# A down projection in Strassen form: ten instead of eight row chunks in each half, two direct chunks, two of the norms ahead of the last product

## The chip, the cores and the metric

One core of a Trainium2 chip runs the whole program. The metric is the device time of one launch in microseconds (us), median of several runs; the kernel before takes 1778.9 us (three runs, 1778.78 to 1779.9).

## What is computed

The reference is a decoder trunk of two layers on 512 tokens of width 1024, all in float32. Each layer is feed-forward, mixer, feed-forward, each followed by a layer norm:

```
def swiglu_ffn(x, w_gu, w_down):
    a, u = jnp.split(x @ w_gu, 2, axis=-1)
    return (jax.nn.silu(a) * u) @ w_down
...
    for l in range(DEPTH):
        x = layer_norm(DEEPNORM_ALPHA * x + 0.5 * swiglu_ffn(x, ffn1_w_gu[l], ffn1_w_down[l]), ln1_g[l], ln1_b[l])
        x = layer_norm(DEEPNORM_ALPHA * x + hybrid_mixer(x, ...), ln2_g[l], ln2_b[l])
        x = layer_norm(DEEPNORM_ALPHA * x + 0.5 * swiglu_ffn(x, ffn2_w_gu[l], ffn2_w_down[l]), ln3_g[l], ln3_b[l])
```

The change concerns the second matrix product of the feed-forward, `h @ w_down`: h is 512 tokens by 2816, w_down is 2816 by 1024. It stands four times in the program (two in each layer).

## The kernel before

**Products.** Every product of two float32 operands is made of three matmuls (`mm3`, lines 171 to 176): both operands are split into a rounded high part and a rest (`split`, line 162: a cast on ScalarE, then a subtraction on VectorE), and high by high, low by high and high by low are summed in PSUM.

**The down projection** (`ffn` from line 638, `down_items` from 348). Of the 22 chunks of 128 rows of w_down, the first 16 (`FIRST`, four `GROUPS` of two chunks in each half) go through Strassen's scheme in Winograd's form: contraction, output columns and tokens are each halved, and seven products (p2, p1, p5, p6, p3, p7, p4 in the order of the loop at 736) stand for eight. One product is four groups, and a group is 12 matmuls with 512 moving columns (`seventh`, 699). The last six chunks are multiplied directly, 24 matmuls a chunk: one ahead of product p4 (line 741), one behind it, and the last four (`TAIL`) token group by token group (756 to 761), 12 matmuls for each half of a token group's row, and behind each token group its norm (`norm`, 459).

**Operands.** The token side is combined in place in `hT` by VectorE (`fifth`, `third`) and split into four slots of `xh` and `xl`, which hold nothing else in this stage (`operand`, 649). The weight side: p2 reads its block from a raw buffer; for the others one tile R holds a block of w_down, and after a group's split GpSimd starts a DMA that adds the next block onto it (line 376, `accum_op=ALU.add`). So between two uses of one R piece there is a split, a DMA of 512 KB and the next split. There are four such sets in each projection: p1 to p5, p5 to p6, p6 to p4 and p3 to p7, with one DMA to a group.

**Order.** `Weights.pump` emits splits of weights up to six units ahead of their use. Everything else is put in order by the scheduler of the language when the program is built, and each engine runs its list in order. Four token groups (t = 0 to 3, 128 tokens each) have their own PSUM banks, two for each (`acc[t][0]`, `acc[t][1]`). The stage that follows needs the normed Y of a token group transposed (`to_xT`, 436: 8 transposes on TensorE, split on ScalarE and VectorE). It begins with the tokens of t = 0 and 1, so that the norms of t = 2 and 3 may finish under it.

Of the kernel before, what the change touches and what calls it, by code (L numbers as in the profile page):

```python
# [18 lines left out]
P = 128  # L19
# [8 lines left out]
SCALE = HD ** -0.5  # L28
TAIL = 4
GROUPS = 4  # L30
FIRST = 4 * GROUPS
SEVEN = (2, 3, 4, 5, 6, 7, 8, 9, 10)
UBUFS = 6
LOOK = 6
DELAY = (4, 3, 9, 9)
STEPS = ((4, 2, 2), (3, 2, 3), (3, 3, 2), (3, 2, 2))
# [59 lines left out]
class Trunk:  # L96
# [64 lines left out]

    def split(self, hi, lo, src, behind=None):
        a = self.nc.scalar.copy(hi, src)  # L163
        b = self.nc.vector.tensor_sub(lo, src, hi.bitcast(F32))  # L164
        if behind is not None:
            self.tc.add_manual_dep(b.ins, behind.ins.name, NOSYNC, reason="the reading goes first")
        if self.pin:
            self.tc.keep_in_program_order(a)
            self.tc.keep_in_program_order(b)
# [94 lines left out]
    def rows_item(self, w, r0, key, pools, heads=False):  # L264

        def load():
            v = self.raw().rearrange("p (c n) -> p c n", c=2)
            if heads:
                for kv in range(2):
                    q0 = kv * 256 + r0 // 2  # L270
                    self.nc.sync.dma_start(v[kv * HD : (kv + 1) * HD],
                                           w[q0 : q0 + P, :].rearrange("(c p) n -> p c n", p=HD))
            else:
                self.nc.sync.dma_start(v, w[r0 : r0 + 256, :].rearrange("(c p) n -> p c n", p=P))
            return v

        def cut(c):
            def go(v, hi, lo):
                self.split(hi, lo, v[:, c, :], self.reading if pools[c] == self.tail_units else None)
# [53 lines left out]
    def ffn_items(self, gu, down, key):  # L333
        items = []
        for fp in range(NFP):
            a = self.cols_item(gu, fp * 256, (key, "a", fp))
            u = self.cols_item(gu, DFF + fp * 256, (key, "u", fp))
            if fp == 0:
                items += [a[0], u[0], a[1], u[1]]
            else:  # L340
                items += self.seven_items(a, u) if fp in SEVEN else a + u
        rows = []
        for fp in range(FIRST // 2, NFP):
            late = [self.tail_units if fp * 2 + c >= NF - TAIL else None for c in range(2)]
            rows += self.rows_item(down, fp * 256, (key, "d", fp), late)
        return items + self.down_items(down, key, rows[0]) + rows[1:]

    def down_items(self, w, key, row):

# [3 lines left out]
        R = {}  # L353
        ms = range(GROUPS // 2)

        def rows(i, j, r, n):
            r0 = i * GROUPS * 256 + r
            return w[r0 : r0 + n, j * 512 : (j + 1) * 512].rearrange("(k p) c -> p k c", p=P)

        def begin(i, place, go):  # L360
            def f(*args):
                pool, tag = place()
                for m in ms:
                    R[i, m] = pool.tile([P, 4, 512], F32, tag=tag, name=self.nm("R"), bufs=2)
                    self.nc.sync.dma_start(R[i, m], rows(i, i, m * 512, 512))
                return go(*args)
            return f

        def cut(t, g, *more):
            def go(v, hi, lo):  # L370
                hv, lv = (t_.rearrange("p (k c) -> p k c", k=2) for t_ in (hi, lo))
                src = R[t, g // 2][:, g % 2 * 2 : g % 2 * 2 + 2, :]
                self.split(hv, lv, src)
                for i, j in more:
                    self.tc.keep_in_program_order(
                        self.nc.gpsimd.dma_start(src, rows(i, j, g * 256, 256), accum_op=ALU.add))  # L376
                return hv, lv
            return go
# [3 lines left out]

        p2 = []
        for m in ms:
            p2 += self.wide_item(w, 0, GROUPS // 2 + m, (key, "b", m))
# [103 lines left out]
    def ffn(self, g_, b, out=None):  # L489
        nc, tc, W = self.nc, self.tc, self.W  # L490
        with ExitStack() as ctx:
# [99 lines left out]
            for fp in range(NFP):  # L591
# [31 lines left out]
                if fp == NFP - 1:  # L623
                    early = W.take()
                    hv = [v.rearrange("p (g f t) -> p g f t", g=2, f=2) for v in early]
                    self.split(*(v.rearrange("p g f t -> p (g f) t") for v in hv), hT[:, 2 * GROUPS : 2 * GROUPS + 4, :256])
                if fp in SEVEN:
# [13 lines left out]

            slots = [0]

            def part(m, i, j):

                f = (j * GROUPS + 2 * m) * 2
                return hT[:, f : f + 4, i * 256 : (i + 1) * 256]

            def operand(src):

                k = slots[0] = (slots[0] + 2) % KC
                f = src.shape[1]
                hh, hl = (v[:, k : k + 2, :].rearrange("p k t -> p (k t)").rearrange("p (f t) -> p f t", f=f)
                          for v in (self.xh, self.xl))
                self.split(hh, hl, src)
                h = f // 2
                return [(hh[:, q * h : q * h + h], hl[:, q * h : q * h + h]) for q in range(2)]

            s1 = pool.tile([P, 4, 256], F32, tag="tlh", name=self.nm("s1"), bufs=TAIL)

            def fifth(m):

                a11, a21, a22 = part(m, 0, 0), part(m, 1, 0), part(m, 1, 1)
                nc.vector.tensor_sub(s1, a21, a22)
                nc.vector.tensor_sub(a21, a11, a21)
                nc.vector.tensor_sub(a11, s1, a11)
                return operand(s1)

# [5 lines left out]
            def operands():  # L674
                ms = range(GROUPS // 2)
                for m in ms[1:]:
# [9 lines left out]
                for m in ms:  # L686
                    yield from operand(part(m, 1, 0))
                chunks = operand(hT[:, FIRST : FIRST + 2, :])
                yield chunks[0]
                for m in ms:  # L690
                    yield from operand(part(m, 1, 1))
                yield chunks[1]
                for f in range(NF - TAIL, NF, 2):
                    room = pool.tile([P, 2, 2, 512], F32R, tag="hr", name=self.nm("hr"), bufs=2)
                    self.split(room[:, 0], room[:, 1], hT[:, f : f + 2, :], self.reading)
                    for q in range(2):
                        yield room[:, 0, q : q + 1], room[:, 1, q : q + 1]

# [17 lines left out]

            def chunk(f):
                u, h = W.get(), ahead.pop(0)
                ahead.append(next(split))
                for i, (t, q) in enumerate(((0, 0), (0, 1), (1, 0), (1, 1), (2, 1), (3, 1), (2, 0), (3, 0))):  # L720
                    down(f, u, h, t, q)
                    if i % 4 == 3:
                        self.step()
                W.done()

# [3 lines left out]
            def into(banks, t0, q, scale, sign=ALU.add):  # L729

                for i, b_ in enumerate(banks):
                    y = self.Y[:, t0 + i, q * 512 : (q + 1) * 512]
                    self.reading = nc.vector.scalar_tensor_tensor(out=y, in0=y, scalar=scale, in1=b_, op0=ALU.mult,
                                                                  op1=sign)

            for n, (banks, new, more) in enumerate((
# [3 lines left out]
                if n == 6:  # L740
                    chunk(FIRST)
                for g in range(GROUPS):
                    u, h = W.get(), ahead.pop(0)
                    ahead.append(next(split))
                    seventh(banks, u, h, new and g == 0)
                    if more and g == GROUPS - 1:
                        into(banks, *more)
                    W.done(2 if n == 0 and g == 1 else 1)
            for f in range(FIRST + 1, NF - TAIL):
                if f == FIRST + 1:  # L750
                    gb = self.load_ln(self.spool, g_, b, "S", 2)
                chunk(f)
            ahead += list(split)
            us = [W.get() for _ in range(TAIL)]
            self.pend = []
            for t in range(NT):
                for q in range(2):
                    for i in range(TAIL):
                        down(NF - TAIL + i, us[i], ahead[i], t, q)
                    self.step()  # L760
                self.norm(t, acc[t], gb, out, DELAY[t], (1.0 if t < 2 else ALPHA, 1.0))

# [387 lines left out]
```

## Time and profile before

| what | value |
|---|---|
| median of three runs | 1778.9 us (1778.78 to 1779.9) |
| the profiled execution | 1778.04 us |
| its span, first to last instruction | 1776.3 us |
| TensorE busy | 1764.0 us, 99% |
| VectorE busy | 1385.9 us, 78% |
| ScalarE busy | 906.9 us, 51% |
| GpSimd busy | 162.4 us, 9% |
| granted TensorE clock, mean | 0.999 |
| HBM traffic | 117 GB/s over the span |

PE is TensorE, DVE VectorE, ACT ScalarE, POOL GpSimd, SP the engine that only issues DMAs. L174 is line 174 of the kernel. A matmul's row gives its modelled duration, which overlaps with the next one; the spacing of the starts is the rate. A VectorE instruction's duration overlaps with the next start in the same way. In a row of the timeline the bracket at the end is the idle time ahead of it on its engine and what ended it.

### The profile page before, as it was taken

The numbers are of one execution on the slowest core, as the hardware profiler recorded it, in microseconds if no ns is written. First come the engines' busy times: TensorE is split into PE (matmuls) and PEld (weight loads), VectorE is DVE, ScalarE is ACT, GpSimd is POOL, SyncE is SP. The second block draws the span as 40 slices with busy tenths as digits, with TensorE's granted clock in tenths as the row PEclk, the third lists the DMA queues.
The fourth block names the chain that finished last, engine by engine and source line by source line (L and its number), as shares of the span: only waits on it lengthen the run. The fifth ranks groups of instructions, "written<-read, shape, count | busy, mean of one in ns | idle before, by whom it ended". The sixth has DMA issues, their size and how long they took to land. (4 is left out here: it accounts for less than half of the span.)

```text
span 1776.3 us, 29093 instructions
## 1 busy us (share of the span) xinstructions
PE 1764.0 (99%) x11978; PEld 1609.5 (91%) x11978; DVE 1385.9 (78%) x1927; ACT 906.9 (51%) x1424; POOL 162.4 (9%) x136
## 2 busy tenths in 40 slices
PE   9999999999999999999999999999999999999998
PEld 9999988887789999998899999889877899999886
DVE  7788888756757788879788887877567587888795
ACT  5455565278712455556235555643795234555550
POOL 0000031111111000012000000301011110000221
PEclk9999999999999999999999999999999999999999
DMA  6234396323222243288412334962233122234871
GB/s 190 96 103 135 120 226 154 113 84 90 74 75 72 84 131 96 96 235 154 156 50 96 117 96 156 225 165 66 84 96 95 48 95 96 96 100 138 226 151 51
DMA packets 158326, 210.07 MB, mean 118 GB/s; under 512 B 4848, under 2 KB 116208, under 8 KB 158192
## 3 DMA queue, kind: packets, MB, share of 16 engines
q1 hardware_dynamic: 140784, 174.64, 30.5%
q0 software_dynamic: 17408, 33.56, 10.6%
q8 instruction: 94, 1.54, 0.4%
q14 instruction: 40, 0.33, 0.1%
HBM read 206.09 MB, written 2.10 MB: 117 GB/s over the span
## 5 line engine op out<-in xcount | busy, mean ns | idle before, releaser
L174 PE MATMUL ps<-xh,uh 128*128 128x256 f32 (+1 forms) x1616 | 482.2, 298 | 0.0
L176 PE MATMUL ps<-xh,ul 128*128 128x256 f32 (+1 forms) x1616 | 479.4, 297 | 0.3 <-DVE ul L164 0.2
L175 PE MATMUL ps<-xl,uh 128*128 128x256 f32 (+1 forms) x1616 | 478.9, 296 | 0.7 <-DVE xl L164 0.5
L163 ACT CAST uh<-raw 128x1024 fp32r<-128x1024 f32 (+1 forms) x286 | 248.3, 892 | 259.1 <-PE ps L175 140.0
L164 DVE TENSOR_TENSOR ul<-raw,uh 128x1024 fp32r<-128x1024 f32 (+1 forms) x286 | 286.5, 1021 | 69.7 <-ACT uh L163 69.1
L174 PE MATMUL ps<-Th,uh 128*128 128x256 f32 x1152 | 319.1, 277 | 0.0
L175 PE MATMUL ps<-Tl,uh 128*128 128x256 f32 x1152 | 318.7, 277 | 0.0
L176 PE MATMUL ps<-Th,ul 128*128 128x256 f32 x1152 | 318.3, 276 | 0.0
L174 PEld LDWEIGHTS ps<-xh,uh 128*128 128x128 f32 x1616 | 308.0, 191 | 9.8 <-issue 1.6
L176 PEld LDWEIGHTS ps<-xh,ul 128*128 128x128 f32 x1616 | 307.9, 191 | 9.4 <-DVE ul L164 0.9
L175 PEld LDWEIGHTS ps<-xl,uh 128*128 128x128 f32 x1616 | 308.0, 191 | 9.1 <-DVE xl L164 1.7
L174 PE MATMUL ps<-uh,xh 128*128 128x512 f32 x672 | 264.3, 393 | 0.5 <-ACT xh L163 0.5
L176 PE MATMUL ps<-uh,xl 128*128 128x512 f32 x672 | 262.0, 390 | 0.0
L175 PE MATMUL ps<-ul,xh 128*128 128x512 f32 x672 | 261.6, 389 | 0.0
L163 ACT CAST uh<-S 128x1024 fp32r<-128x1024 f32 x144 | 151.1, 1050 | 149.1 <-PE ps L175 145.2
L164 DVE TENSOR_TENSOR ul<-S,uh 128x1024 fp32r<-128x1024 f32 x144 | 175.9, 1222 | 60.0 <-ACT uh L163 59.3
L174 PEld LDWEIGHTS ps<-Th,uh 128*128 128x128 f32 x1152 | 216.7, 188 | 0.0
L175 PEld LDWEIGHTS ps<-Tl,uh 128*128 128x128 f32 x1152 | 216.7, 188 | 0.0
L176 PEld LDWEIGHTS ps<-Th,ul 128*128 128x128 f32 x1152 | 216.4, 188 | 0.0
L376 POOL DMA_DIRECT2D R<-in_ffn_w_down_dram x64 | 77.8, 1221 | 983.0 <-DVE ul L164 952.2
L174 PEld LDWEIGHTS ps<-uh,xh 128*128 128x128 f32 x672 | 126.2, 188 | 28.2 <-issue 1.6
L176 PEld LDWEIGHTS ps<-uh,xl 128*128 128x128 f32 x672 | 126.1, 188 | 27.3 <-DVE xl L164 0.9
(143 smaller groups left out, 2388.7 us busy)
## 6 DMA issues: line engine op xcount, KB each, us to landing
raw<-in_ffn_w_gu_dram SPq DMA_DIRECT2D x86, 1024.0 KB, 5.7
R<-in_ffn_w_down_dram POOLq DMA_DIRECT2D x64, 512.0 KB, 7.3
raw<-in_ffn_w_down_dram SPq DMA_DIRECT2D x20, 1024.0 KB, 5.0
raw<-in_w_in_dram SPq DMA_DIRECT2D x18, 1024.0 KB, 5.2
R<-in_ffn_w_down_dram SPq DMA_DIRECT2D x16, 1024.0 KB, 6.4
raw<-in_w_in_dram SPq DMA_DIRECT2D x8, 512.0 KB, 5.1
raw<-in_w_out_dram SPq DMA_DIRECT2D x8, 512.0 KB, 6.1
raw<-in_w_out_dram SPq DMA_DIRECT2D x4, 1024.0 KB, 5.0
```

The costliest lines, as they stand in the source:

```text
L163: a = self.nc.scalar.copy(hi, src)
L164: b = self.nc.vector.tensor_sub(lo, src, hi.bitcast(F32))
L174: keep(mm(out, ah, bh, start=start, stop=False, **kw))
L175: keep(mm(out, ah, bl, start=False, stop=False, **kw))
L176: keep(mm(out, al, bh, start=False, stop=stop, **kw))
L376: self.nc.gpsimd.dma_start(src, rows(i, j, g * 256, 256), accum_op=ALU.add))
```

## The change

`GROUPS` goes from 4 to 5, so that 20 chunks take the seven products and two (`TAIL`) are direct. A half of ten chunks is handled in three pieces of 4, 4 and 2 chunks (`PAIRS`). The accumulating DMAs become five to a set, 20 instead of 16 in each projection. The two direct chunks of token groups 0 and 1 and their norms now stand ahead of p4, and those of token groups 2 and 3 behind it. The norm's two vectors are loaded at the start of the projection, into its own pool. The line that held one reading of PSUM ahead of a split (`behind`) goes. In the changed kernel the lines are shifted: split is 163 to 166, the accumulating DMA 374, the norm 485 to 497, the reading of a product's banks 747.

```diff
-TAIL = 4
-GROUPS = 4
-FIRST = 4 * GROUPS
+TAIL = 2
+GROUPS = 5
+HALF = 2 * GROUPS
+FIRST = 2 * HALF
+PAIRS = [(m, min(4, HALF - m)) for m in range(0, HALF, 4)]
...
-DELAY = (4, 3, 9, 9)
+DELAY = (5, 4, 9, 9)
...
-        return items + self.down_items(down, key, rows[0]) + rows[1:]
+        return items + self.down_items(down, key, tail)
...
+        def plain(m):
+            k0, n = PAIRS[m]
+
+            def load():
+                v = self.raw()[:, : n * 512].rearrange("p (k c) -> p k c", k=n)
+                self.nc.sync.dma_start(v, rows(1, 0, k0, n))
+                return v
...
+        p2 = [item for m in range(len(PAIRS)) for item in plain(m)]
         p1, p5, p6, p4 = product(0, (0, 1)), product(0, (1, 1)), product(0, (1, 0)), product(0)
         p3, p7 = product(1, (0, 1)), product(1)
-        p2[2] = p2[2][:3] + (begin(0, lambda: (self.spool, "S"), p2[2][3]),)
-        p5[0] = p5[0][:3] + (begin(1, lambda: (self.fpool, "hr"), p5[0][3]),)
-        return p2 + p1 + p5 + p6 + p3 + p7 + [row] + p4
+        for m in range(2):
+            hook(p2, 2, 0, m, lambda: (self.spool, "S"))
+            hook(p5, 0, 1, m, lambda: (self.fpool, "hr"))
+        hook(p1, 1, 0, 2, lambda: (self.fpool, "r"))
+        hook(p5, 0, 1, 2, lambda: (self.fpool, "r"))
+        return p2 + p1 + p5 + p6 + p3 + p7 + tail + p4
...
+            gb = self.load_ln(pool, g_, b)
+            calls = [0]
...
-                k = slots[0] = (slots[0] + 2) % KC
+                calls[0] += 1
+                k, h = ((4, 0), (0, 0), (0, 1), (4, 1))[calls[0] % 4 if calls[0] < 20 else 2]
                 f = src.shape[1]
-                hh, hl = (v[:, k : k + 2, :].rearrange("p k t -> p (k t)").rearrange("p (f t) -> p f t", f=f)
-                          for v in (self.xh, self.xl))
+                hh, hl = (v[:, k : k + f, h * 256 : (h + 1) * 256] for v in (self.xh, self.xl))
                 self.split(hh, hl, src)
...
+            def tail(t):
+                for q in range(2):
+                    for i, (u, h) in enumerate(last):
+                        down(FIRST + i, u, h, t, q)
+                    self.step()
+                self.norm(t, acc[t], gb, out, DELAY[t], (1.0 if t < 2 else ALPHA, 1.0))
...
                 if n == 6:
-                    chunk(FIRST)
+                    last = [take() for _ in range(TAIL)]
+                    self.pend = []
+                    for t in range(2):
+                        tail(t)
                 for g in range(GROUPS):
...
-            for f in range(FIRST + 1, NF - TAIL):
-                if f == FIRST + 1:
-                    gb = self.load_ln(self.spool, g_, b, "S", 2)
-                chunk(f)
-            ahead += list(split)
-            us = [W.get() for _ in range(TAIL)]
-            self.pend = []
-            for t in range(NT):
-                for q in range(2):
-                    for i in range(TAIL):
-                        down(NF - TAIL + i, us[i], ahead[i], t, q)
-                    self.step()
-                self.norm(t, acc[t], gb, out, DELAY[t], (1.0 if t < 2 else ALPHA, 1.0))
+            for t in range(2, NT):
+                tail(t)
```

On TensorE the built program has 11422 rows where the one before has 11470.

What VectorE runs at three places, in its order. In the names `ul` is the low part of a weight unit, `raw` a weight buffer filled by DMA, `R` the accumulated tile, `xl` the low part of a token-side operand or of the transposed input, `ps` a PSUM bank, `Y` the residual stream, `ln` the norm's vectors, `S` a sum of weights for the next feed-forward.

First place: VectorE around the last product of the first feed-forward. Before:

```order
L164 TENSOR_TENSOR ul_3301<-raw_3238,uh_3300 128x1024
L164 TENSOR_TENSOR ul_3320<-raw_3238,uh_3319 128x1024
L164 TENSOR_TENSOR ul_3339<-raw_3286,uh_3338 128x1024
L164 TENSOR_TENSOR ul_3373<-raw_3286,uh_3372 128x1024
L164 TENSOR_TENSOR ul_3380<-raw_3323,uh_3379 128x1024
L164 TENSOR_TENSOR ul_3384<-raw_3323,uh_3383 128x1024
L164 TENSOR_TENSOR ul_3390<-raw_3376,uh_3389 128x1024
L164 TENSOR_TENSOR ul_3607<-raw_3376,uh_3606 128x1024
L466 SCALAR_TENSOR_TENSOR Y<-Y,ps_2780 128x512
L468 BN_STATS st_3417<-Y 128x6
L466 SCALAR_TENSOR_TENSOR Y<-Y,ps_2781 128x512
```

Now:

```order
L166 TENSOR_TENSOR ul_3368<-R_2828,uh_3367 128x1024
L747 SCALAR_TENSOR_TENSOR Y<-Y,ps_2785 128x512
L747 SCALAR_TENSOR_TENSOR Y<-Y,ps_2787 128x512
L166 TENSOR_TENSOR ul_3424<-raw_2772,uh_3423 128x1024
L485 SCALAR_TENSOR_TENSOR Y<-Y,ps_2781 128x512
L485 SCALAR_TENSOR_TENSOR Y<-Y,ps_2782 128x512
L487 BN_STATS st_3385<-Y 128x6 x2
L485 SCALAR_TENSOR_TENSOR Y<-Y,ps_2783 128x512
L489 BN_AGGR mv_3390<-st_3385 128x2
```

The norm of token group 0 stood behind all splits of the stage and six splits of the next one; now it stands behind the readings of p7 (L747) and the last split of p4's weights (R_2828), and the splits of the next stage's weights (raw_2772 and later) stand between the steps of the norms.

Second place: VectorE where a feed-forward follows a feed-forward, at the norm of token group 3. Before:

```order
L475 SCALAR_TENSOR_TENSOR Y<-Y,mv_8992,ln_8774 128x1024
L582 SCALAR_TENSOR_TENSOR hT_9012<-ps_9022,Q_9071 128x256
L478 SCALAR_TENSOR_TENSOR Y<-Y,rs_8996,ln_8774 128x1024
L306 TENSOR_TENSOR S_9341<-raw_9019 128x512
L310 TENSOR_TENSOR S_9341<-raw_9019 128x512
```

Now:

```order
L306 TENSOR_TENSOR S_9379<-raw_8992 128x512
L489 BN_AGGR mv_9036<-st_9031 128x2
L310 TENSOR_TENSOR S_9379<-raw_8992 128x512
L491 TENSOR_SCALAR ve_9038<-mv_9036 128x1
L494 SCALAR_TENSOR_TENSOR Y<-Y,mv_9036,ln_8241 128x1024
L307 TENSOR_TENSOR S_9379<-S_9379,raw_8992 128x512
L497 SCALAR_TENSOR_TENSOR Y<-Y,rs_9040,ln_8241 128x1024
```

Three of the sums S now stand ahead of the last step of that norm (L497, before L478); they stood behind it.

Third place: VectorE at the end of the program, where the two last norms begin. Before:

```order
L475 SCALAR_TENSOR_TENSOR Y<-Y,mv_17710,ln_17611 128x1024
L466 SCALAR_TENSOR_TENSOR Y<-Y,ps_17062 128x512
L478 SCALAR_TENSOR_TENSOR Y<-Y,rs_17714,ln_17611 128x512 x2
L468 BN_STATS st_17745<-Y 128x6
L466 SCALAR_TENSOR_TENSOR Y<-Y,ps_17063 128x512
```

Now:

```order
L494 SCALAR_TENSOR_TENSOR Y<-Y,mv_17748,ln_17122 128x1024
L497 SCALAR_TENSOR_TENSOR Y<-Y,rs_17752,ln_17122 128x512 x2
L485 SCALAR_TENSOR_TENSOR Y<-Y,ps_17118 128x512
L487 BN_STATS st_17833<-Y 128x6
L485 SCALAR_TENSOR_TENSOR Y<-Y,ps_17119 128x512
```

The first reading for token group 2 (ps_17062, now ps_17118) stood inside the norm of token group 1; now that norm is finished ahead of it. The two last norms themselves are laced into each other as before.

## Rows read from the trace of the kernel before

**Rows 1.** The page: the span, and part 1, busy time by engine.

```profile
span 1776.3 us, 29093 instructions
...
PE 1764.0 (99%) x11978; PEld 1609.5 (91%) x11978; DVE 1385.9 (78%) x1927; ACT 906.9 (51%) x1424; POOL 162.4 (9%) x136
```

**Rows 2.** Groups by line and shape: a 512-column matmul, busy us, mean ns, idle time ahead.

```profile
L174 PE MATMUL ps<-uh,xh 128*128 128x512 f32 x672 | 264.3, 393 | 0.5 <-ACT xh L163 0.5
```

**Rows 3.** Timeline of PE: first and last of the program's last 96 matmuls.

```profile
1746.28 0.39 PE L174 MATMUL ps<-uh,hr 128*128 128x512 f32 x1
...
1767.83 0.39 PE L176 MATMUL ps<-uh,hr 128*128 128x512 f32 x1
```

**Rows 4.** Busy time by stretch: the first down projection, clock, DMA share, GB/s.

```profile
core 0: us, PE busy (x) PEld busy (x) DVE busy (x) ACT busy (x) POOL busy (x), PEclk, DMA share, GB/s
234.00:345.00 111.00, 111.00 (x507) 92.41 (x506) 92.14 (x98) 49.82 (x52) 24.13 (x19) 1.00 0.72 170
```

**Rows 5.** Timeline of DVE: two splits back to back, and the next start.

```profile
264.69 2.35 DVE L164 TENSOR_TENSOR xl<-hT,xh 128x1024 fp32r<-128x1024 f32 x2
266.96 1.22 DVE L164 TENSOR_TENSOR ul<-R,uh 128x1024 fp32r<-128x1024 f32 x1
```

**Rows 6.** Timeline of DVE: the end of the program.

```profile
1749.21 0.69 DVE L466 SCALAR_TENSOR_TENSOR Y<-Y,ps 128x512 f32<-128x512 f32 x1 [12.99 <-PE ps L176]
...
1760.37 0.68 DVE L466 SCALAR_TENSOR_TENSOR Y<-Y,ps 128x512 f32<-128x512 f32 x1
1760.96 1.41 DVE L478 SCALAR_TENSOR_TENSOR Y<-Y,rs,ln 128x512 f32<-128x512 f32 x2
1762.29 0.69 DVE L468 BATCH_NORM_STATS2 st<-Y 128x6 f32<-128x512 f32 x1
...
1765.84 0.68 DVE L466 SCALAR_TENSOR_TENSOR Y<-Y,ps 128x512 f32<-128x512 f32 x1
...
1771.83 1.42 DVE L478 SCALAR_TENSOR_TENSOR Y<-Y,rs,ln 128x512 f32<-128x512 f32 x2 [0.44 <-POOL rs L474]
```

**Rows 7.** Timeline of PE: the first matmul of the first down projection.

```profile
232.39 0.39 PE L174 MATMUL ps<-uh,uh 128*128 128x512 f32 x1
```

**Rows 8.** Timeline of POOL: the accumulating DMAs of the first projection (16 in all).

```profile
236.24 1.35 POOL L376 DMA_DIRECT2D R<-in_ffn_w_down_dram  x1 [234.93 <-DVE ul L164]
...
240.75 1.20 POOL L376 DMA_DIRECT2D R<-in_ffn_w_down_dram  x1 [1.05 <-DVE ul L164]
246.43 1.23 POOL L376 DMA_DIRECT2D R<-in_ffn_w_down_dram  x1 [4.48 <-DMA R<-in_ffn_w_down_dram]
...
277.74 1.22 POOL L376 DMA_DIRECT2D R<-in_ffn_w_down_dram  x1 [0.98 <-DVE ul L164]
```

**Rows 9.** Line 376: issue to landing of the 64 accumulating DMAs.

```profile
DMA to landing us min/median/max: 5.7/7.3/11.2
```

**Rows 10.** DMA, 210 to 290 us in 40 slices of 2 us.

```profile
DMA  9996808729328999999999999999999999999300
GB/s 274 401 369 194 330 1 219 305 33 348 152 33 289 406 391 306 247 214 208 209 202 210 201 214 204 182 204 207 200 183 200 204 201 195 205 201 199 73 0 0
```

**Rows 11.** DMA issues, 222 to 262 us: KB each, median us to landing.

```profile
R<-in_ffn_w_down_dram SPq DMA_DIRECT2D x2, 1024.0 KB, 9.2
```

**Rows 12.** The page, part 6: the same loads over the whole program.

```profile
R<-in_ffn_w_down_dram SPq DMA_DIRECT2D x16, 1024.0 KB, 6.4
```

**Rows 13.** Timeline of DVE where a feed-forward follows a feed-forward.

```profile
897.85 1.28 DVE L478 SCALAR_TENSOR_TENSOR Y<-Y,rs,ln 128x1024 f32<-128x1024 f32 x1
899.17 0.69 DVE L306 TENSOR_TENSOR S<-raw 128x512 f32<-128x512 f32 x1
899.78 0.68 DVE L310 TENSOR_TENSOR S<-raw 128x512 f32<-128x512 f32 x1
```

**Rows 14.** Timeline of PE at the same place: 256-column matmuls, then transposes.

```profile
900.10 0.28 PE L174 MATMUL ps<-xh,uh 128*128 128x256 f32 x1
...
901.54 1.91 PE L442 MATMUL ps<-ident,Y 128*128 128x128 f32 x16
```

More of the change, by code (lines that the diff above doesn't have):

```diff
@@ L160, in units, with split @@
         return hi, lo
-    def split(self, hi, lo, src, behind=None):
+    def split(self, hi, lo, src):
         a = self.nc.scalar.copy(hi, src)
         b = self.nc.vector.tensor_sub(lo, src, hi.bitcast(F32))
-        if behind is not None:
-            self.tc.add_manual_dep(b.ins, behind.ins.name, NOSYNC, reason="the reading goes first")
         if self.pin:
@@ L278, in go @@
             def go(v, hi, lo):
-                self.split(hi, lo, v[:, c, :], self.reading if pools[c] == self.tail_units else None)
+                self.split(hi, lo, v[:, c, :])
                 return hi, lo
@@ L375, in go @@
                     self.tc.keep_in_program_order(
-                        self.nc.gpsimd.dma_start(src, rows(i, j, g * 256, 256), accum_op=ALU.add))
+                        self.nc.gpsimd.dma_start(src, rows(i, j, g * 2, 2), accum_op=ALU.add))
                 return hv, lv
@@ L625, in ffn @@
                     hv = [v.rearrange("p (g f t) -> p g f t", g=2, f=2) for v in early]
-                    self.split(*(v.rearrange("p g f t -> p (g f) t") for v in hv), hT[:, 2 * GROUPS : 2 * GROUPS + 4, :256])
+                    self.split(*(v.rearrange("p g f t -> p (g f) t") for v in hv), hT[:, HALF : HALF + 4, :256])
                 if fp in SEVEN:
@@ L674, in operands @@
             def operands():
-                ms = range(GROUPS // 2)
+                ms = range(len(PAIRS))
                 for m in ms[1:]:
@@ L687, in operands @@
                     yield from operand(part(m, 1, 0))
-                chunks = operand(hT[:, FIRST : FIRST + 2, :])
-                yield chunks[0]
+                room = pool.tile([P, 2, TAIL, 512], F32R, tag="hr", name=self.nm("hr"), bufs=2)
+                self.split(room[:, 0], room[:, 1], hT[:, FIRST:, :])
+                for q in range(TAIL):
+                    yield room[:, 0, q : q + 1], room[:, 1, q : q + 1]
                 for m in ms:
                     yield from operand(part(m, 1, 1))
[L692 to L695, printed above, removed]
-                    for q in range(2):
-                        yield room[:, 0, q : q + 1], room[:, 1, q : q + 1]
             def seventh(banks, u, h, new):
@@ L715, in ffn, with take @@
             ahead = [(hv[0][:, g], hv[1][:, g]) for g in range(2)] + [next(split)]
-            def chunk(f):
+            def take():
                 u, h = W.get(), ahead.pop(0)
[L719 to L722, printed above, removed]
-                        self.step()
-                W.done()
+                ahead.append(next(split, None))
+                return u, h
             low, high = [acc[t][0] for t in (2, 3)], [acc[t][1] for t in (2, 3)]
@@ L740, in ffn @@
                 if n == 6:
-                    chunk(FIRST)
+                    last = [take() for _ in range(TAIL)]
+                    self.pend = []
+                    for t in range(2):
+                        tail(t)
                 for g in range(GROUPS):
-                    u, h = W.get(), ahead.pop(0)
-                    ahead.append(next(split))
+                    u, h = take()
                     seventh(banks, u, h, new and g == 0)
```

55 lines of the change are left out of this document (28 added, 27 removed).

## The prediction, on record ahead of the result

> **What bounds the kernel now.** I read the share of busy time first: TensorE is busy 1764.0 of 1776.3 us, VectorE 1385.9, the rest far less [rows 1]. An average does not say whether TensorE is also never kept waiting, so next come the groups by line: the 672 high-by-high matmuls with 512 columns have 0.5 us of idle time ahead of them in the whole program [rows 2]. [...] So every matmul taken away is worth its spacing, as long as what feeds TensorE keeps its lead. Two things could lose it: VectorE, with 18.9 us to spare in 111, and the accumulating DMAs, during which the DMA engines are at nine tenths or more from about 236 to 284 us [rows 10]. The one place where TensorE does not set the time is the end of the program, so I read VectorE's timeline there too [rows 6].
>
> **The matmuls.** Four more direct chunks go into the scheme. They took 4 x 24 = 96 matmuls; as a fifth group in each of seven products they take 7 x 12 = 84. That is 12 fewer in a projection, 48 in the program, as the row counts on TensorE say (11470 to 11422). The spacing comes from the last 96 matmuls: 1767.83 - 1746.28 = 21.55 us for 95 steps, 0.2268 us [rows 3]. So 12 x 0.2268 = 2.72 us a projection and **-10.9 us** in all, while no new wait appears. A group of 12 takes 2.72 us; a product takes 13.6 instead of 10.9, seven take 95.3.
>
> **VectorE inside the projection.** In units of 1024 elements: weight splits rise by 7 x 1 and fall by 4 (direct chunks), 3 more; operand splits go from 17 to 18.5; the combinations in `fifth` and `third` go from 2 pieces to 2.5 at four operations each, 2 more. These 6.5 start every 1.14 us ((266.96 - 264.69) / 2, [rows 5]): 7.4 us more on an engine with 18.9 us idle, in a stage 2.7 us shorter. The norms of token groups 0 and 1 were in the stage before and still are. VectorE is left with some 9 us idle and has no queue that grows; cost nothing, covered by TensorE's own 95 us.
>
> **The norms ahead of p4.** One norm occupies VectorE for 1765.84 - 1760.37 = 5.47 us [rows 6]. Two need 10.9 us; p4 behind the direct chunks gives 13.6 us. What waits on VectorE behind these norms is the split of p4's last operand piece, used in its fifth group, and the next stage's splits. By VectorE's order and these durations the piece's split comes some 11 us behind the readings of p7, and TensorE needs it 5.4 + 4 x 2.72 = 16.3 us behind them. Cost nothing; without the cover it is the 5 us between.
>
> **Accumulating DMAs.** Each projection issues 20 instead of 16 on POOL. The 16 took from 236.24 to 277.74, 2.77 us each, three in flight at a time (the fourth, at 246.43, waited for a landing) [rows 8]; the last lands a median 7.3 us after issue [rows 9], at 285.0. Product p7, which needs the last set, began at 232.39 + 5 x 10.9 = 286.7 [rows 7], its last group 8.2 us later, and a group's split should be done 2.2 us ahead (a cast and a subtraction): a lead of about 8 us. After the change the first issue is some 3.5 us later (239.8; VectorE has three more operations of 1.14 us ahead of it), the last 19 steps on, 239.8 + 19 x 2.77 = 292.4, landed at 299.7. The last group of p7 begins at 232.39 + 5 x 13.6 + 10.9 = 311.3; its limit is 309: a lead of 9.4 us. Against this stand loads that the change brings into the stretch: the next stage's first 1 MB of weights, 1 MB of norm vectors and three 0.5 MB pieces where there were none, about 3.1 MB; at the 400 GB/s that plain loads reach [rows 10] 7.8 us. All of that lateness in one chain leaves 1.6 us. So the cost is nothing at the lower end; at the upper, with the 3.4 us a step of the first three issues (246.43 - 236.24, [rows 8]) kept up for all 19, the last lands at 311.7, 2.7 us late in each projection. I take nothing, since 12 of the 15 steps were at the faster rate.
>
> Plain loads and accumulations do share: the two R loads issued among the accumulations took 9.2 us [rows 11], against 6.4 over the program [rows 12]. [...]
>
> **The boundaries.** Behind the last two direct parts (24 matmuls, 5.4 us) the next stage starts on tokens whose transposes were made inside p4. After a feed-forward the next one runs 96 matmuls of 256 columns at 0.12 us ((901.54 - 900.10) / 12, [rows 14]), 11.5 us, before it transposes token groups 2 and 3: 16.9 us from the start of those direct parts. VectorE reads the first of their banks after 6 matmuls and 0.21 us (1.57 us; the 0.21 from 1749.21 - 1746.28 - 12 x 0.2268, [rows 3, 6]), works two norms (10.9) plus their last step (1.3), and three sums of 0.61 us [rows 13] that now stand ahead of that step: 15.6. Splits of the next weights ahead of them can hold VectorE for one or two operations more, 16.7 to 17.9. Before, the norm was done at 899.13 and the transposes began at 901.54 [rows 13, 14], 2.4 us of slack. I take **+0.4 us** for this one boundary (bounds 0 and 2). Towards the mixer there are 24 more matmuls between, 2.9 us: nothing, twice.
>
> **The end of the program.** Before, the last direct matmul is issued at 1768.06 and the span ends at 1776.3: 8.2 us exposed. After, the last 24 matmuls take 5.44 us, the first reading starts 1.57 us into them, and from the reading of token group 2 to the last L478 the trace has 1771.83 + 1.42 - 1760.37 = 12.88 us, of which 1.33 (1762.29 - 1760.96) belong to the norm before it, now finished earlier: 11.55. Behind the last step come 3.05 us of output [rows 6]. 1.57 + 11.55 + 3.05 = 16.2 us, 10.7 of them exposed: **+2.5 us**. Bounds: nothing, if the two norms hid as before, and one norm, 5.5.
>
> **Sum.** -10.9 + 0.4 + 2.5 = -8.0 us. The profiled execution took 1778.04 us, 0.9 below the median of 1778.9; against the median I forecast **1770.9 us**, 0.45% less.
>
> **The rivals.**
> Full gain: the end costs nothing more because the two last norms are laced more tightly. Then -10.9, 1768.0 us. For it: POOL and TensorE leave VectorE free there. Against: VectorE is solid in the last 24 us [rows 6], with two norms and only 5.4 us of matmuls to hide them.
> Partly lost: the norms of token groups 2 and 3, or the accumulations, are late by 0.5 to 2 us at several of the places with little lead. With 1 us in each of four projections -4, 1774.9; with 2 us at the three boundaries -2, 1776.9. For it: leads of 1.6 and about 0 us. Against: those leads add every unfavourable bound.
> Slower: the accumulating DMAs become the bound of p7. Each step of i us lands the last at 239.8 + 19i + 7.3; TensorE waits 19i - 61.9 us in each projection, and the gain of 8.0 / 4 = 2.0 us is gone at i = 3.36. At 3.6 it waits 6.5 us in each, 26 in all: 1797 us. For it: 3.4 us a step while plain loads ran. Against: 2.61 in the 12 steps behind them, since 277.74 - 246.43 = 31.3 [rows 8].
> That the change doesn't do what it says is excluded by the row count on TensorE.
>
> **The numbers.** The forecast 0.64, full gain 0.08, partly lost 0.20, slower 0.08. The range from 1767.6 to 1776.0 holds the first two, the forecast's bounds (end 0 to 5.5, boundary 0 to 2) and about half of the partly lost. A measurement here tells 0.2% from no change, 3.6 us. Faster by more: 0.64 + 0.08 + half of 0.20 = 0.82. Same: the other half and 0.01 of the slower case, 0.11. Slower: 0.07.
>
> **What would show it.** Right: the spacing stays at 0.227 us, TensorE is busy without a gap through seven products of 13.6 us, each projection is 2.7 us shorter, the last L497 ends about 7.6 us behind the last matmul's issue, where it was 5.2. Wrong: a wait of TensorE for a split `ul` of an R tile with a DMA behind it (the accumulations), or for transposes of token groups 2 and 3 (the boundaries), or POOL steps above 3.3 us.

## The result, and the profile after

The changed kernel takes 1785.25 us (median of six runs, 1782.59 to 1788.07) against 1779.16 us for the kernel before on the same chip (six runs, 1778.78 to 1779.9): a ratio of 1.0033, 95% interval 1.002 to 1.0046, 6.1 us **slower**. The forecast was 1770.9 us, and its range ended at 1776.0. The profiled execution took 1784.17 us, 6.1 more than the one before. Two single runs of later kernels, one of `e6_transposes_later` (2919.5 us, granted clock 0.56) and one of `e8_four_ahead` (1916.7 us, 0.85), ran in a slow state and are no part of the comparisons.

The first view below answers to [rows 1]. The second is the group of 512-column matmuls whose token side is a low part (`xl`); its columns are those of [rows 2].

```profile
span 1782.4 us, 29182 instructions
...
PE 1758.7 (99%) x11930; PEld 1603.4 (90%) x11930; DVE 1414.1 (79%) x1975; ACT 926.9 (52%) x1456; POOL 181.8 (10%) x152
```

```profile
L176 PE MATMUL ps<-uh,xl 128*128 128x512 f32 x720 | 283.2, 393 | 9.3 <-DVE xl L166 9.3
```

TensorE's matmuls fell as forecast (11978 to 11930), but in front of one group of them it stood 9.3 us, waiting for VectorE's `xl`. The timeline of PE shows where: in the third product, p5, of each projection, at its fifth group, the one whose token-side operand is the new 2-chunk piece.

```profile
271.06 0.39 PE L175 MATMUL ps<-ul,xh 128*128 128x512 f32 x1
274.15 0.50 PE L176 MATMUL ps<-uh,xl 128*128 128x512 f32 x1 [2.70 <-DVE xl L166]
...
275.83 0.63 PE L176 MATMUL ps<-uh,xl 128*128 128x512 f32 x1
276.26 0.63 PE L174 MATMUL ps<-uh,xh 128*128 128x512 f32 x1
```

The other three projections have the same row with waits of 2.73, 3.19 and 0.68 us. Behind the wait the spacing is 0.43 us instead of 0.227. Busy time by stretch, in the columns of [rows 4], shows that the granted clock has fallen to 0.50:

```profile
272.00:274.00 2.00, 0.00 (x0) 0.00 (x0) 1.73 (x2) 1.45 (x3) 0.66 (x2) 1.00 1.15 209
274.00:276.00 2.00, 1.85 (x7) 1.54 (x8) 2.00 (x3) 2.00 (x3) 1.15 (x1) 0.85 1.12 205
276.00:278.00 2.00, 2.00 (x7) 1.51 (x6) 2.00 (x3) 1.30 (x2) 1.22 (x1) 0.50 1.12 205
278.00:280.00 2.00, 2.00 (x9) 1.59 (x8) 2.00 (x4) 1.21 (x2) 0.97 (x1) 0.80 1.15 210
```

The missing clock is 2 x (0.15 + 0.50 + 0.20) = 1.7 us here. In the third projection it is 3.1 us, counted from the end of the wait (0.50 from 1156.7 to some 1162.8 us), and in the other two nothing.

The end of the program went as forecast: the last matmul's row and the last step of the last norm are

```profile
1771.41 0.39 PE L176 MATMUL ps<-uh,hr 128*128 128x512 f32 x1
```

```profile
1777.73 1.41 DVE L497 SCALAR_TENSOR_TENSOR Y<-Y,rs,ln 128x512 f32<-128x512 f32 x2 [0.44 <-POOL rs L493]
```

so 1782.4 - 1771.41 = 10.99 us stand behind the last matmul's start, where it was 1776.3 - 1767.83 = 8.47 [rows 1, 3].

| from the span of before to that after | us |
|---|---|
| 48 matmuls fewer | -10.9 |
| end of the program | +2.5 |
| four waits in p5 | +9.3 |
| lower clock behind two of them | +4.8 |
| ahead of the first projection (232.39 to 232.74, same order there) | +0.35 |
| sum | +6.05 |

The spans differ by 6.1 us: in sum, nothing of size is missing.

**Why `xl` is late.** VectorE's timeline ahead of the wait:

```profile
264.59 0.68 DVE L686 TENSOR_TENSOR s<-hT 128x512 f32<-128x512 f32 x1
265.19 1.22 DVE L693 TENSOR_TENSOR hT<-hT 128x1024 f32<-128x1024 f32 x1
267.17 1.23 DVE L166 TENSOR_TENSOR ul<-R,uh 128x1024 fp32r<-128x1024 f32 x1 [0.77 <-ACT uh L165]
268.31 1.28 DVE L747 SCALAR_TENSOR_TENSOR Y<-Y,ps 128x512 f32<-128x512 f32 x2
269.51 0.68 DVE L687 TENSOR_TENSOR hT<-hT 128x512 f32<-128x512 f32 x1
270.11 1.22 DVE L166 TENSOR_TENSOR ul<-R,uh 128x1024 fp32r<-128x1024 f32 x1
271.25 0.68 DVE L688 TENSOR_TENSOR hT<-s,hT 128x512 f32<-128x512 f32 x1
272.27 1.23 DVE L166 TENSOR_TENSOR ul<-R,uh 128x1024 fp32r<-128x1024 f32 x1 [0.34 <-ACT uh L165]
273.41 0.68 DVE L166 TENSOR_TENSOR xl<-s,xh 128x512 fp32r<-128x512 f32 x1
```

The sum `s` that the piece needs is done at 265.3, and its cast `xh` at 267.67, as ScalarE's timeline says. Its `xl` runs at 273.41, because three splits of R, two of them for the next product, stand ahead of it in VectorE's list, with two readings of PSUM and two combinations in `hT` between them. The last of the three has its cast at 271.19, and that waits for an accumulating DMA. On POOL, below it, these DMAs are issued 3.6 to 5.2 us apart from 249.7 to 266.3 us; in [rows 8] the sixteen took 2.77 each.

```profile
267.05 0.62 ACT L165 CAST xh<-s 128x512 fp32r<-128x512 f32 x1
...
271.19 1.04 ACT L165 CAST uh<-R 128x1024 fp32r<-128x1024 f32 x1 [1.50 <-DMA R<-in_ffn_w_down_dram]
```

```profile
239.12 1.35 POOL L374 DMA_DIRECT2D R<-in_ffn_w_down_dram  x1 [237.81 <-DVE ul L166]
...
249.73 1.23 POOL L374 DMA_DIRECT2D R<-in_ffn_w_down_dram  x1 [5.93 <-DVE xl L166]
253.78 1.21 POOL L374 DMA_DIRECT2D R<-in_ffn_w_down_dram  x1 [2.82 <-DVE s L686]
258.94 1.20 POOL L374 DMA_DIRECT2D R<-in_ffn_w_down_dram  x1 [3.95 <-DVE xl L166]
262.53 1.20 POOL L374 DMA_DIRECT2D R<-in_ffn_w_down_dram  x1 [2.38 <-DVE hT L688]
266.31 1.22 POOL L374 DMA_DIRECT2D R<-in_ffn_w_down_dram  x1 [2.58 <-issue]
268.85 1.21 POOL L374 DMA_DIRECT2D R<-in_ffn_w_down_dram  x1 [1.32 <-DVE ul L166]
...
301.26 1.22 POOL L374 DMA_DIRECT2D R<-in_ffn_w_down_dram  x1 [1.94 <-issue]
```

And SP's queue shows what runs beside them: the next stage's weights, the norm's vectors and four R pieces within 5 us, 1 + 1 + 3 MB.

```profile
235.28 0.37 SPq L195 DMA_DIRECT2D raw<-in_w_in_dram  x1
235.69 0.57 SPq L474 DMA_DIRECT2D ln<-in_ln_g_dram  x1
236.32 0.42 SPq L475 DMA_DIRECT2D ln<-in_ln_b_dram  x1
236.78 3.24 SPq L363 DMA_DIRECT2D R<-in_ffn_w_down_dram  x4
```

That makes theory A: late DMAs, passed on by the order of VectorE's list. Its rivals: VectorE has simply too much work (B); the cost is the reordering of the norms (C); the late DMAs hold TensorE by themselves (D).

### The profile page after: what moved, and what is told of

It is laid out like the page before. It is cut to its first block, busy times and chain, and to the rows that moved or that the text cites. A ratio compares the mean times of both kernels' runs of the same rounds, so it can differ in the third digit from the quotient of the medians.

```text
span 1782.4 us, 29182 instructions
## 1 busy us (share of the span) xinstructions
PE 1758.7 (99%) x11930; PEld 1603.4 (90%) x11930; DVE 1414.1 (79%) x1975; ACT 926.9 (52%) x1456; POOL 181.8 (10%) x152
## 4 chain that ended last, share of the span: by engine, by line
PE 79%; issue 10%; DMA 4%; DVE 3%; POOL 2%; ACT 1%; POOLq 0%; SPq 0%; DVEq 0%; ACTq 0%
PE ps L176 25%; PE ps L174 25%; PE ps L175 25%; DMA R<-in_ffn_w_down_dram 2%; POOL R L374 1%; DVE ul L166 1%; PE ps L461 1%; DMA raw<-in_ffn_w_gu_dram 1%; POOL sw L932 1%; PE ps L1040 1%; ACT uh L165 1%; PE ps L988 0%; PE ps L1002 0%; PE ps L1036 0%; DVE hT L596 0%
## 5 line engine op out<-in xcount | busy, mean ns | idle before, releaser
L165 ACT CAST uh<-raw 128x1024 fp32r<-128x1024 f32 (+1 forms) x274 | 237.6, 886 | 229.0 <-PE ps L175 134.4
L166 DVE TENSOR_TENSOR ul<-raw,uh 128x1024 fp32r<-128x1024 f32 (+1 forms) x274 | 273.5, 1012 | 42.0 <-ACT uh L165 41.2
L176 PE MATMUL ps<-uh,xl 128*128 128x512 f32 x720 | 283.2, 393 | 9.3 <-DVE xl L166 9.3
L174 PE MATMUL ps<-uh,xh 128*128 128x512 f32 x720 | 285.4, 396 | 0.5 <-ACT xh L165 0.5
L175 PE MATMUL ps<-ul,xh 128*128 128x512 f32 x720 | 282.0, 392 | 0.0
L374 POOL DMA_DIRECT2D R<-in_ffn_w_down_dram x80 | 97.1, 1217 | 1046.1 <-DVE ul L166 719.6
L165 ACT CAST uh<-R 128x1024 fp32r<-128x1024 f32 x120 | 124.4, 1047 | 125.0 <-DMA R<-in_ffn_w_down_dram 92.9
L166 DVE TENSOR_TENSOR ul<-R,uh 128x1024 fp32r<-128x1024 f32 x120 | 144.7, 1220 | 54.6 <-ACT uh L165 54.4
```

The lines of the kernel that those rows point to most:

```text
L174: keep(mm(out, ah, bh, start=start, stop=False, **kw))
L175: keep(mm(out, ah, bl, start=False, stop=False, **kw))
L176: keep(mm(out, al, bh, start=False, stop=stop, **kw))
L374: self.nc.gpsimd.dma_start(src, rows(i, j, g * 2, 2), accum_op=ALU.add))
```

## The experiments

All times are medians against the kernel before on the same chip (1779.39, 1778.91 and 1779.59 us in the three groups of four).

**1. Loads later** (`e1_loads_later`), and **2. operands earlier** (`e2_operands_earlier`), and **3. both** (`e3_both`).

```diff
-            for r2, l2, _, _ in self.items[self.emitted :]:
+            for r2, l2, _, _ in self.items[self.emitted : self.emitted + 16]:
...
-            gb = self.load_ln(pool, g_, b)
+                        if n == 2:      # behind into(banks, *more)
+                            gb.append(self.load_ln(pool, g_, b, after=self.Y[:, 1, 1023:]))
```

(`after`: a copy of one column of Y into the tile, so that the loads wait for p5's readings.) The second kernel:

```diff
-            ahead = [...] + [next(split)]
+            ahead = [...] + [next(split) for _ in range(3)]
```

In the second and third, p4's last operand piece is written into the slot of its first while that is still to be used, so p4's first two groups multiply other data; all else is as it was.

> Holds back three loads of 1 MB each that the change let run among the first accumulating DMAs: the norm's vectors (now behind the readings of the third product, p5), the rows of the direct chunks and the first weights of the next stage (now 16 units ahead of use). Theory A: TensorE's 2.7 us wait for the low part of p5's last operand piece comes from VectorE's list, in which that piece stands behind two splits of R whose DMAs are late because of these plain loads. Then the first accumulating DMAs step by 3.3 us or less instead of about 3.9, the wait shrinks to under 0.5 us in each projection, the clock stays at 1.00, and the time falls by the 9.3 us of waits and the some 4.8 us that the lower clock cost, to about 1771 us. Rival B: VectorE simply has too much to do ahead of that piece; then at least 2 us of wait stay in each projection and the time stays above 1780 us.

> The loads stay as the change has them; token-side operands are asked for five groups ahead of use instead of three, so that VectorE works p5's last piece ahead of the two splits of R. Theory A: the steps of the accumulating DMAs stay at 3.6 us and more until 266 us, but TensorE no longer waits for the piece (under 0.3 us in each projection), and nothing else is late, because those two splits are needed only 5 to 8 us later: about 1771 us. Rival B (VectorE has too much to do): the wait moves to another operand, of 1.5 us or more in each projection, and the time stays above 1778 us. Rival D: the accumulating DMAs are late enough to hold TensorE by themselves at the next product; then a wait for the low part of a weight unit takes the place of the one that went.

> Both edits of the two runs before. Theory A: each alone is enough, so the two together give no more than the better of them, about 1771 us, no wait above 0.3 us in a projection. If two causes add up (late DMAs at the start and a late piece), this one is faster than either alone by 2 us or more.

Measured: 1775.3 us (ratio 0.9974, 0.9962 to 0.9985), 1776.31 (0.9984, 0.9975 to 0.9993), 1775.94 (0.998, 0.9971 to 0.9989). Each edit alone takes the wait in p5 away, down to 0.38 us and less in the first kernel and to nothing in the second; B falls, since VectorE's busy time is unchanged (1413.1 and 1412.8 us), and D too: the 720 matmuls on a low part of weights (`ul`, `xh`) have 0.0 us of idle time ahead of them in all three kernels. Both edits together give no more than one alone. The second kernel is the clearest: its loads and its POOL steps are as late as in the change (253.89, 259.19, 263.11, 266.77), only the place in VectorE's list is another, ahead of the readings L747 and of two splits of R:

```profile
268.77 0.69 DVE L687 TENSOR_TENSOR hT<-hT 128x512 f32<-128x512 f32 x1
269.37 0.69 DVE L166 TENSOR_TENSOR xl<-s,xh 128x512 fp32r<-128x512 f32 x1
...
270.58 1.28 DVE L747 SCALAR_TENSOR_TENSOR Y<-Y,ps 128x512 f32<-128x512 f32 x2
271.77 1.22 DVE L166 TENSOR_TENSOR ul<-R,uh 128x1024 fp32r<-128x1024 f32 x1
```

Two misses. The times are 4 to 5 us above the 1771 expected: a second wait comes up (experiment 6), and the second and third kernels have new waits of up to 0.64 us at `xl` pieces of p7. And the first kernel did not do what its expectation says. On SP's queue the direct rows are issued at 232.91 us and the next stage's weights at 236.44, against 232.67 and 235.28 in the change: only the vectors were held back (282.17).

**4. All four norms behind p4** (`e4_norms_behind`): undoes the reordering.

```diff
-                    for t in range(2):
-                        tail(t)
...
-            for t in range(2, NT):
+            for t in range(NT):
                 tail(t)
```

> The change with the direct chunks and norms of token groups 0 and 1 put back behind the last product p4, so that all four norms stand there. If the reordering is what costs, the time falls below 1785 us. By the prediction's terms it should rise: 48 matmuls, 10.9 us, now cover four norms of 5.5 us; at the end of the program 1.6 + 4 x 5.5 + 3.0 - 10.9 = 15.7 us stay exposed instead of 10.8, 5 us more, and at each of the three boundaries the next stage waits 2 to 5 us for its first transposes: 1796 to 1805 us. The waits in p5 stay as they are, 2.7 us.

Measured: 1815.66 us, ratio 1.0205 (1.0191 to 1.0219). C falls: the reordering is needed. The waits in p5 are unchanged (9.3 us in the same group). The last matmul starts at 1797.39 of 1813.0 us: 15.6 us exposed, the expected 15.7. The boundaries cost more than expected, 7 to 10 us each against the change: a wait for the norm, one for the split of its transposes, and a lower clock behind them (0.988 over the run).

```profile
347.73 1.09 PE L461 MATMUL ps<-ident,Y 128*128 128x128 f32 x8 [2.39 <-DVE Y L497]
349.06 0.39 PE L174 MATMUL ps<-xh,uh 128*128 128x256 f32 x1 [0.24 <-ACT xh L165]
351.45 0.58 PE L175 MATMUL ps<-xl,uh 128*128 128x256 f32 x1 [2.00 <-DVE xl L166]
```

**5. Which loads?** Only the vectors held back (`e5_vectors_later`: experiment 1 without its first edit, the 16); the vectors behind the R pieces on the queue, without a wait (`e10_vectors_behind`, the first diff); the vectors held back and other bytes in their place (`e11_other_bytes`, the second):

```diff
-            gb = self.load_ln(pool, g_, b)
...
+                if n == 2:
+                    gb.append(self.load_ln(pool, g_, b))
```

```diff
+            for i in range(2):
+                nc.sync.dma_start(room_ln[:, i, :], self.rows0[i * P : (i + 1) * P, :])
```

> Of the three loads that the first run held back, only the norm's vectors (1 MB, two DMAs) are held back here; the rows of the direct chunks and the next stage's first weights run early, as in the change. If the wait in p5 is set by how many bytes run among the first accumulating DMAs (theory A), it lies between the 2.7 to 3.2 us of the change (6 MB) and the 0 to 0.4 us with 3 MB held back: 1 MB at the 400 GB/s of plain loads is 2.5 us of the DMA engines' time, so about 0.5 to 1 us of wait is left in each of the first three projections and the time is 1776 to 1779 us. If one of the other two loads does it alone (rival: a matter of which transfer, not of bytes), the wait stays above 2.3 us and the time above 1782 us.

> The change with the loads of the norm's vectors written later, without a wait: on SP's queue they now stand behind the four loads of R pieces instead of ahead of them, and are issued some 2 us later, still among the first accumulating DMAs. If the place in the queue matters (the fifth piece of R for p1 and the pieces for p3 came late behind the vectors), TensorE's wait in p5 goes as it did with the vectors held back, under 0.7 us in each projection, and the time is 1773 to 1775 us. If it is the bytes in flight, all 6 MB are still there and the waits of 2.7 us stay: above 1782 us.

> The vectors are held back as in the run that held back only them (no wait in p5, 1773.4 us), and in their old place two DMAs of 512 KB load rows of w_down that nobody uses into the same tile. If any 1 MB of plain load there makes the accumulating DMAs late, the waits come back (2.7 us in p5, about 1785 us). If it is something of the vectors' own transfers (one row of memory read 128 times), they do not come back: below 1776 us.

Measured: 1773.42 us (ratio 0.997, 0.9959 to 0.998), 1779.88 (0.9999, 0.999 to 1.0008) and 1782.39 (1.0016, 1.0007 to 1.0024). The group of p5's wait in each, in that order:

```profile
L176 PE MATMUL ps<-uh,xl 128*128 128x512 f32 x720 | 281.1, 390 | 0.6 <-DVE xl L166 0.6
```

```profile
L176 PE MATMUL ps<-uh,xl 128*128 128x512 f32 x720 | 282.5, 392 | 6.7 <-DVE xl L166 6.7
```

```profile
L176 PE MATMUL ps<-uh,xl 128*128 128x512 f32 x720 | 282.6, 393 | 7.0 <-DVE xl L166 6.8
```

It is for the most part the bytes that run among the first accumulating DMAs, in these runs the vectors or unused rows, ahead of the R pieces on the queue or behind them: unused rows in place of the vectors bring most of the wait back (2.03, 2.09 and 2.71 us, where the change has 2.70, 2.73 and 3.19), and so do the vectors behind the R pieces (2.21, 2.07, 2.37). The times of these two stay below the 1785 and 1782 us expected, since part of the wait is gone. The change itself holds the same comparison: its last projection has no next stage and so 1 MB less, and its wait is 0.68 us. With only the vectors held back, VectorE's list around the piece is in the same order as in the change, and its `xl` stands there at

```profile
271.24 0.68 DVE L166 TENSOR_TENSOR xl<-s,xh 128x512 fp32r<-128x512 f32 x1
```

which is 37.4 us behind the projection's start (233.80) instead of 40.7 (273.41 - 232.74), 3.2 earlier. The ninth accumulating DMA is issued 36.1 us behind that start in the change (268.85 - 232.74) and 32.9 here (266.70 - 233.80), also 3.2 earlier, and so the wait of 2.7 us is gone. Of the wait, 0.5 to 1 us was expected to stay in each of three projections; 0, 0 and 0.64 us did. The expectation had priced 1 MB at 2.5 us, at the 400 GB/s of plain loads alone; at the 286 GB/s that all queues together moved in the change from 234 to 266 us it is 3.5 by estimate, and the 3.2 measured lies between. Experiment 1 held back the same loads, and on SP's queue it differs only in the order of the next stage's load and the R pieces; it is 4.1 us under before where this one is 5.5.

So the 1 MB on SP's queue moved POOL's ninth accumulating DMA by 3.2 us in these runs. And VectorE kept to its list: in the change it stood idle 0.34 us ahead of the split at 272.27 while the `xl` behind it had had its `s` and `xh` since 267.67.

**6. Transposes later** (`e6_transposes_later`). In experiment 1 TensorE stood 0.65, 1.04 and 1.15 us at the transposes of token group 1 inside p4, since a split of the next stage's weights stands ahead of the norm's last step (L500 there):

```profile
330.97 1.22 DVE L166 TENSOR_TENSOR ul<-raw,uh 128x1024 fp32r<-128x1024 f32 x1
332.11 1.27 DVE L500 SCALAR_TENSOR_TENSOR Y<-Y,rs,ln 128x1024 f32<-128x1024 f32 x1
```

```profile
333.44 1.09 PE L461 MATMUL ps<-ident,Y 128*128 128x128 f32 x8 [0.65 <-DVE Y L500]
```

```diff
-DELAY = (5, 4, 9, 9)
+DELAY = (5, 5, 9, 9)
```

> The first run (three loads held back) with the transposes of token group 1 one step later inside p4 (DELAY 5, 5 instead of 5, 4). There TensorE stood 0.65, 1.04 and 1.15 us at these transposes, because VectorE had the last step of that norm behind splits of the next stage's weights. Theory: the norms ahead of p4 are not free, they are late by about 1 us; one step, 2.7 us, is enough to hide them, and the time falls by 2.5 us against the first run, to about 1773 us. Rival: the transposes are then late for the next stage, whose first matmuls wait for the split of them instead (1 us or more at each boundary), and the time stays at 1775 us or rises.

Measured: 1774.12 us (ratio 0.9971, 0.9961 to 0.9981), 4.8 us under before where experiment 1 was 4.1 under: 0.7 gained, not 2.5. In the profiled execution (1771.58, the lowest of its runs) all three waits are gone, and one of 0.46 us is left at the transposes where a feed-forward follows a feed-forward. Its projections start 2.69, 2.04 and 2.33 us closer than before, against 2.72 by the matmuls alone.

**7. p4 token by token** (`e7_token_by_token`, and with operands four groups ahead `e8_four_ahead`), then **only at the end** (`e9_end_by_token`; with the vectors alone held back `e12_end_vectors_only`).

```diff
+                    us = [take() for _ in range(GROUPS)]
+                    for i in range(2):
+                        ts = slice(i * P, (i + 1) * P)
+                        for g, (u, h) in enumerate(us):
+                            for f in range(2):
+                                self.mm3(banks[i], (h[0][:, f, ts], h[1][:, f, ts]), ...)
...
+                        tail(2 + i)
```

The first two stand on experiment 6, and p4's last operand piece has a tile of its own; the second has one more `next(split)` ahead. In the third the lines stand under `if out is not None:`, again on experiment 6; the last is the same without the limit of 16.

> The kernel of the run before, and p4 taken token group by token group: all five groups and the direct chunks for t = 2, its norm, then the same for t = 3, with p4's last operand piece in a tile of its own. The prediction put the loss at the end of the program down to two norms behind 24 matmuls (10.8 us exposed in the change). With 42 matmuls, 9.5 us, behind the norm of t = 2 only one norm is left: 0.4 + 4.9 + 3.05 = about 8.3 us exposed, 2.5 us less, and nothing at the boundaries: about 1770.5 us. Rival: p4's five weight units stay occupied, the next stage's splits come late, and TensorE waits for them by 1 us or more at each of three boundaries: 1773 us and more.

> The kernel of the run before, and operands asked for four groups ahead instead of three. If the waits of 0.2 to 0.4 us that the first run still shows at operand pieces in p5 and p7 have the same cause (a piece behind splits of R in VectorE's list), they go, and the time falls by up to 1 us. With five ahead, two projections showed a new wait of 0.63 us at p7 instead; if four ahead shows it too, the time stays as in the run before.

> The run with later transposes, and p4 token group by token group only in the last feed-forward, where no stage follows whose weights would need p4's unit buffers. The run that did it everywhere was 2.3 us shorter from the last projection's start to the end (114.56 us against 116.90) and lost 4 us at each boundary. Theory: the end is a matter of how many norms stand behind the last matmuls; then 1774.1 - 2.4 = about 1771.7 us. Rival: the gain at the end came from something else in that kernel; then 1774 us.

> As the first kernel of this group, but of the loads only the vectors are held back (no limit of 16 units). The trace of the run with that limit shows the next stage's first weights issued at 236.6 us instead of 236.3, so the limit did nearly nothing: the same time as the first kernel of this group within 1 us. If the order of the R pieces and that load on the queue matters, the two differ by more.

Everywhere: 1778.04 us (0.9998, 0.9989 to 1.0006) and 1778.9 (1.0001, 0.9992 to 1.001); the second shows the new wait of 0.63 us at p7 twice, and the time stays, as its expectation has it. In both the rival won: the end gains 2.3 us, and each boundary loses 4, with waits such as this one in the next stage and 0.50 of the clock behind it (the expectation's "weight units" were not it; the wait is for the transposed tokens):

```profile
359.08 0.38 PE L174 MATMUL ps<-xh,uh 128*128 128x256 f32 x1 [1.26 <-ACT xh L165]
```

At the end alone: 1770.99 us (0.9951, 0.9939 to 0.9964) and **1768.92 us** (five runs, 1768.83 to 1770.18; ratio 0.9942, 0.993 to 0.9955), 10.7 us under the kernel before and so some 17 under the change, which was 6.1 over it. The two differ by 2.1 us, not by under 1; their traces differ most in the wait where a feed-forward follows a feed-forward, 1.11 against 0.30 us. Experiments 1 and 5 differ by the same edit and 1.4 us the same way, so the order of those loads on the queue seems to matter; how was not looked into. Of the faster:

```profile
span 1767.0 us, 29194 instructions
```

```profile
L176 PE MATMUL ps<-uh,xl 128*128 128x512 f32 x720 | 280.9, 390 | 0.0
```

```profile
232.00:345.00 113.00, 113.00 (x529) 94.55 (x528) 98.12 (x112) 56.89 (x64) 28.92 (x23) 1.00 0.82 194
```

TensorE is busy 113.00 of 113.00 us in the first projection, at the full clock, with VectorE's 98.12; the last matmul starts 8.5 us ahead of the end (1758.48).

## Why the prediction was wrong

- **The matmuls** (-10.9 us): right. The kernel with the waits taken away and the end restored is 10.7 us faster than before by the medians; in the profiled executions, from the first projection's start to the end, it is 10.4 us (1767.0 - 233.45 against 1776.3 - 232.39), with 0.5 us of waits left where a feed-forward follows a feed-forward.
- **The end** (+2.5 us): right, 10.99 against 8.47 us exposed. The reckoning by norms and covering matmuls also gave experiment 4's 15.7 (15.6).
- **VectorE inside the projection** ("has no queue that grows; cost nothing"): **this is the step that failed.** It compared busy sums, 7.4 us of work against 18.9 us idle [rows 4], and VectorE was indeed never short of time: from 246 to 273 us of the change it stood idle 0.3 to 1.7 us ahead of seven of eight splits of R. But it worked its list in order (0.34 us idle ahead of the split at 272.27, with the `xl` behind that split ready to run), and an urgent operand, the `xl` of the new 2-chunk piece asked for three groups ahead of use, stood behind splits that are made up to six units ahead of use and wait for DMAs. It cost 9.3 us of waits and 4.8 of clock. The order alone put right took the wait in p5 away (experiment 2), and so did the DMAs alone (experiment 5).
- **The accumulating DMAs**: the lead of p7, which the prediction worked out, held; no matmul waited for an R tile. But lateness was weighed only against TensorE's need of the last piece, not against who else stands in VectorE's list meanwhile. The extra loads were counted (3.1 MB, 7.8 us; the items listed make 3.5 MB, 8.8 us, and a lead of 0.6 us instead of 1.6) and then judged by that one deadline. From 239.12 to 301.26 us the 20 DMAs took 3.27 us a step, above the 2.77 taken and near the 3.36 at which the slower rival had the gain used up.
- **The norms ahead of p4** ("cost nothing"): wrong by 2.8 us in experiment 1 and 3.4 in experiment 2, hidden in the change, where TensorE was late itself, and open in the kernels where it was not (experiments 1 to 3 and 5). The splits of the next stage, named there as what waits behind the norms, in fact stand between their steps.
- **The boundary** (+0.4): nothing in the change, 0.3 to 1.1 us in the later kernels; inside its bounds.
- **The rivals**: slower had 0.07, with another mechanism (p7 starved of R). What was to show the prediction wrong was a wait for `ul` of R or POOL steps above 3.3 us; it was a wait for `xl`, behind that `ul`, and the steps, 3.27 us in the mean, were 3.9 in the mean up to 266.3 us and above 3.3 at two places behind it.

What stays open: how the DMA engines divide their time between plain loads and accumulations, what the order of the loads does, and what the runs of one kernel differ in (experiment 6: 1771.58 to 1774.68 us).

## What to carry to other kernels

Where engines work fixed lists, a spare share of busy time is no cover (in the change VectorE was busy 79% of the span, and TensorE waited 9.3 us for its `xl`): for each urgent instruction read what stands ahead of it in its engine's order, and what the slowest of those waits for. Loads that are not needed yet belong behind a wait of their own when a dependent chain of DMAs runs beside them: the vectors held back behind a wait took the kernel from 6.1 us over the one before to 5.5 under; the same loads only put behind the R pieces left it 0.3 over. Past the first wait that goes, look for the next, which it hid (0.65 to 1.15 us at the transposes in experiment 1).

## What the runs showed of the hardware

In these runs a wait of TensorE cost more than its length, but not always. After waits of 2.70 and 3.19 us in the change, 2.21 and 2.37 in `e10_vectors_behind`, 2.09 and 2.71 in `e11_other_bytes` and 1.26 (with 0.34 right behind it) in `e7_token_by_token` the granted clock fell to 0.50 for some 3 to 6 us; after 2.73 in the change, 2.07 in `e10_vectors_behind` and 2.03 in `e11_other_bytes` it stayed at 1.00. The length of a wait alone does not tell which: 2.09 us was followed by 0.50, and 2.73 was not. In the change the wait of 2.73 us thus cost 2.7, and that of 2.70 cost 4.4, which fits the wider spread of the changed kernel's runs (5.5 us against 1.1): those with a granted clock of 0.996 and 0.997 took 1782.6 to 1782.8 us, those with 0.994 and 0.995 1784.2 to 1788.1. That was not tested by itself.
